# A two-layer transformer block on one core: a spread of sums one step on, a weight split ahead of the squares, one more empty step ahead of MLA's transposes

## The chip, the core and the metric

The kernel runs on one core of a Trainium2 chip. The metric is the device time of one execution in microseconds (us). The kernel before took 1670.65 us, the median of 3 runs (1670.29 to 1670.98).

Engines are named as in the profile: PE is TensorE's matmul, PEld its weight load, DVE is VectorE, ACT is ScalarE, POOL is GpSimd, SP is SyncE, which issues most of the DMAs. PSUM banks take the results of PE. Every engine takes its instructions in the order of the program.

## What is computed

Two layers of a hybrid block over 512 tokens of width 1024, in 32-bit floats. Only what the change lies near is kept here:

```python
def rms_norm(x, g):
    xf = x.astype(jnp.float32)
    y = xf * lax.rsqrt(jnp.mean(xf * xf, axis=-1, keepdims=True) + RMS_EPS)
    return (y * g.astype(jnp.float32)).astype(x.dtype)

def reference(x, w_in, ...):
    for l in range(DEPTH):
        h = rms_norm(x, g_pre_mix[l])
        mix = hybrid_mixer(h, w_in[l], ...)
        x = x + rms_norm(mix, g_post_mix[l])
        h = rms_norm(x, g_pre_ffn[l])
        f = (jax.nn.silu(h @ w_ffn_gate[l]) * (h @ w_ffn_up[l])) @ w_ffn_down[l]
        x = x + rms_norm(f, g_post_ffn[l])
    return x

def hybrid_mixer(h, w_in, ...):
    (fq, fk, fv, ff, dq, dk, dv, rq, rk, rv, rg, cq, ckv, kr) = jnp.split(h @ w_in, IN_OFFSETS, axis=-1)
    ...
    q = heads(rms_norm(cq, mla_q_norm) @ w_uq, MLA_HEADS)
    kv = heads(rms_norm(ckv, mla_kv_norm) @ w_ukv, MLA_HEADS)
    ...
```

The mixer holds four attentions (forgetting, dilated, retention, and MLA, whose queries and keys come from the small latents `cq`, `ckv`, `kr`), and gates that weigh them.

## The kernel before, in words

**Matmuls.** Every operand is split into a high part (a rounded copy) and a low part (what is left), and every product is three matmuls: high by high, high by low, low by high. For a weight, ACT makes the high part (line 290) and DVE the low part (line 291). The weights are a stream of plan entries. `w_conv(i)` splits entries up to number `i`, each by `conversion`, which first issues the load of the entry two further on (SP, line 259, three `raw` buffers) and then two casts on ACT and two subtractions on DVE. `take` hands out the next entry, with `self.wi` its number; `w_conv(self.wi)` therefore splits the entry that is to be taken next.

**Order.** Between `ordered(True)` and `ordered(False)` PE, ACT, DVE and POOL run in the order in which the code is written; elsewhere a scheduler sets the order. The written order covers the start of the program (`first_block`, `latents`) and the border of the layers (`down_block`, `latents`). SP's order is left to the scheduler at the border.

**The border of the layers.** `down_block` ends layer 0. The last of the eight columns of the FFN is computed in two halves of 256 tokens. For a half, `sums` adds the squares of the tokens on PE (line 571) and DVE makes a factor of them (lines 588 to 563); `start` spreads the factor over the partitions by two small matmuls on PE (`spread`, line 601); `renewal` then makes from it the new `x` and the split operands `u[k]` of the next layer: DVE lines 1344 and 1350, POOL line 1346, ACT line 1348. Beside it runs `latent_steps`, the product for layer 1's latents (lines 1037 to 1039): first for token blocks 0 and 1 with k from 0 to 7, six matmuls for each k, then for token blocks 2 and 3. What is done ahead of which k stands in a table `at`; the half of the first tokens is renewed by then, and the table places the sums and the spread of the second half:

```python
        at = {0: [...], 1: [...],
              EA: [lambda: sums(1), ...],
              ES: [lambda: start(1), lambda: some(g[1], 4)]}
```

with `EA, ES = 2, 5`. Token blocks 2 and 3 read the second half's operands. Once the renewal is issued, `squares()` (made by `squares_and_factors`) issues the squares of the new `x` (`square_sums`: eight squares on ACT, lines 1331 and 1334; six additions on DVE, line 1335, and one, line 1067), the split of the first `dq` weight, and an activation that loads nothing at the border but in layer 0 fetches ACT's table for the square root. `self.factors` comes in `latents` after the first of the eight k of `dq` (`TQ = 1`): it sums these squares per token on PE (line 571) and makes layer 1's factor. In the first layer `first_block` calls the same two functions with the input as `x`.

**After it.** `latents` squares the latents on ACT (line 1196), makes their factors on DVE, spreads layer 1's factor on PE (line 601, after five k of `dq` in layer 1), copies the spread on ACT (line 1076), splits the second `dq` weight, and only then scales the latents on DVE (lines 1213 to 1217).

**MLA's preparation.** `mla_prepare` is a generator that is worked off beside the columns of the projections: `collect` takes one step of the oldest background generator each time that enough columns have been issued (`SPACING = 6.5`). Its first steps split `uq` and `ukv` and rotate `kr` (DVE lines 878 to 882); the next ones transpose the latents on PE (lines 889, 895, 902). Behind it in the same queue stand MLA's attention, then the dilated, the forgetting and the retention one. In an attention, line 673 makes scores, 682 to 692 the normalised exponentials (DVE, ACT, POOL), 699 transposes them, 709 and 710 split them (ACT, DVE), 753 multiplies with the values. Scores, transposes and products take turns on the four PSUM banks named `b`.

Of the kernel before, what the change touches and what calls it, by code (L numbers as in the profile page):

```python
# [40 lines left out]


DA, DS, CQ, D0 = 4, 10, 9, 2
EA, ES = 2, 5

TQ, QT, QT1 = 1, 2, 5

# [161 lines left out]
class Builder:  # L209
# [657 lines left out]
    def mla_prepare(self, l, cq, ck, res):  # L867
        nc = self.nc
        ident = self.con("ident")
        uq = [self.split(self.up.pop(0)) for _ in range(2)]  # L870
        yield
        ukv = self.split(self.up.pop(0))
        for p in range(2):
            c = ck[p][:, 0:384].rearrange("p (t c) -> p t c", t=2)
            cs = slice(64 * p, 64 * p + 64)
            cos = self.con("tcos")[:, cs].rearrange("p (t c) -> p t c", t=2)
            sin = self.con("tsin")[:, cs].rearrange("p (t c) -> p t c", t=2)
            nc.vector.tensor_mul(c[:, :, 160:176], c[:, :, 144:160], sin[:, :, 0:16])
            nc.vector.tensor_mul(c[:, :, 176:192], c[:, :, 128:144], sin[:, :, 16:32])
            nc.vector.tensor_mul(c[:, :, 128:160], c[:, :, 128:160], cos)  # L880
            nc.vector.tensor_add(c[:, :, 160:192], c[:, :, 128:160], c[:, :, 160:192])
            nc.vector.tensor_copy(c[:, :, 128:160], c[:, :, 160:192])
        yield
        cqT, ckT = [], []
        for kb in range(2):
            tp = self.ps("b")
            for t in range(4):
                o = 256 * (t % 2) + 128 * kb
                nc.tensor.transpose(tp[:, 128 * t:128 * t + 128], cq[t // 2][:, o:o + 128], ident)
            self.defer(lambda tp=tp, kb=kb: cqT.append(self.split(tp, scale=self.vec("qn", 2 * l + kb))))  # L890
            yield
        tp = self.ps("b")
        for t in range(4):
            o = 192 * (t % 2)
            nc.tensor.transpose(tp[:, 128 * t:128 * t + 128], ck[t // 2][:, o:o + 128], ident)
        self.defer(lambda tp=tp: ckT.extend(self.split(tp, scale=self.vec("kvn", l))))
        yield
        K = [(self.ar(), self.ar()) for _ in range(4)]
        tp = self.ps("b")
        for t in range(4):  # L900
            o = 192 * (t % 2) + 64
            nc.tensor.transpose(tp[:, 128 * t:128 * t + 128], ck[t // 2][:, o:o + 128], ident)

        def shared():

            hi, lo = (t[64:128, :] for t in K[0])
            nc.scalar.copy(hi, tp[64:128, :])
            nc.vector.tensor_sub(lo, tp[64:128, :], hi.bitcast(F32))
            for h in range(1, 4):
                for p in range(2):  # L910
                    self.move(K[h][p][64:128, :], K[0][p][64:128, :])
        self.defer(shared)
        yield
        yield
        Q = []

        def q_out(ps):

            f = self.a()
            nc.vector.tensor_mul(f, ps, self.con("mrope"))  # L920
            Q.append(self.split(f))

        for h in range(4):
            ps = self.ps("b")
            for kb in range(2):
                w = [uq[kb][p][:, 128 * h:128 * h + 128] for p in range(2)]
                self.mm3(ps, w, cqT[kb], kb == 0, kb == 1)
            self.defer(lambda ps=ps: q_out(ps))
            yield
            ps = self.ps("b")  # L930
            self.mm3(ps[0:64, :], [ukv[p][:, 128 * h:128 * h + 64] for p in range(2)], ckT, True, True)
            self.defer(lambda ps=ps, h=h: self.split_to(K[h][0][0:64, :], K[h][1][0:64, :], ps[0:64, :]))
            yield
        for t in range(4):
            ts = slice(128 * t, 128 * t + 128)
            if t % 2 == 0:
                ps = self.ps("b")
            half = ps[:, 256 * (t % 2):256 * (t % 2) + 256]
            o = half.rearrange("p (h d) -> p h d", h=4)
            w = [ukv[p].rearrange("p (h d) -> p h d", h=4)[:, :, 64:128] for p in range(2)]  # L940
            nc.tensor.matmul(o, ckT[0][:, ts], w[0], start=True, stop=False)
            nc.tensor.matmul(o, ckT[0][:, ts], w[1], start=False, stop=False)
            nc.tensor.matmul(o, ckT[1][:, ts], w[0], start=False, stop=True)
            self.defer(lambda half=half: res["v"].append(self.v_split(half)))
            if t % 2 == 1:
                yield
                yield
        self.flush()
        for h in range(4):
            (q0, q1), (k0, k1) = Q[h], K[h]  # L950
            res["qk"].append(((q0, k0), (q0, k1), (q1, k0)))
# [184 lines left out]
    def squares_and_factors(self):  # L1136

        nc = self.nc
        part = []

        def squares():
            part.append(self.square_sums())
            self.w_conv(self.wi)
            nc.scalar.activation(self.small(1), part[0][:, 0:1], AF.Sqrt)
        return squares, lambda: self.next_factors(self.token_sums(part[0]))

# [865 lines left out]
```

## Time and profile before

The profiled execution took 1670.84 us, of which the span from the first to the last instruction is 1669.0 us.

| | |
|---|---|
| median of 3 runs | 1670.65 us |
| profiled execution, its span | 1670.84 us, 1669.0 us |
| busy: PE, PEld | 1647.4 us (99%), 1462.5 us (88%) |
| busy: DVE, ACT, POOL | 1135.7 us (68%), 849.8 us (51%), 357.9 us (21%) |
| chain that ended last | PE 91%, DVE 5%, issue 2%, ACT 1%, POOL 1%, DMA 1% |

PE is busy nearly all the time, so time can be gained only where PE waits, or where its clock is down. In the rows below, a time in brackets is the idle time of the engine ahead of the instruction and what ended it. The granted clock of PE is given as a share of 2.4 GHz.

### The profile page before, as it was taken

Reading aid. Unit: us, or ns where it says so; the run is one execution under the profiler, and the core shown is the slowest. Engines: PE = TensorE matmul, PEld = TensorE weight load, DVE = VectorE, ACT = ScalarE, POOL = GpSimd, SP = SyncE. Lnnn points to the kernel's source line nnn. Section 1 sums busy time; section 2 is a strip of 40 time slices with the busy share of each in tenths; the row PEclk is TensorE's granted clock in tenths of the full one; section 3 lists DMA queues with packets and bytes.
Section 4 is the critical chain, followed back from the end, with each engine's and each line's share of the span. In section 5 each row is a group of like instructions: output and inputs, shape, how many; then the busy total and the mean of one; then the engine's idle time right before and its main releaser. Section 6 shows DMA issues by size and latency. Waiting matters only on the chain.

```text
span 1669.0 us, 26499 instructions
## 1 busy us (share of the span) xinstructions
PE 1647.4 (99%) x9746; PEld 1462.5 (88%) x9746; DVE 1135.7 (68%) x2165; ACT 849.8 (51%) x1682; POOL 357.9 (21%) x400
## 2 busy tenths in 40 slices
PE   9999999999999999999999999999999999999997
PEld 7898888888899999988888988888888989999876
DVE  7657676746569777762286576767464687777897
ACT  7566553323456555553265665533333565555655
POOL 0234333432130001000122343334311300000000
PEclk9999999999999999999999999999999999999999
DMA  6645225767735777443246442257666247775572
GB/s 220 162 108 144 77 89 174 178 173 179 205 104 138 187 181 186 99 152 97 76 149 164 113 138 76 95 170 177 174 156 180 73 139 196 185 187 150 187 238 90
DMA packets 93697, 248.88 MB, mean 149 GB/s; under 512 B 11520, under 2 KB 23040, under 8 KB 93568
## 3 DMA queue, kind: packets, MB, share of 16 engines
q1 hardware_dynamic: 72768, 205.24, 39.5%
q0 software_dynamic: 20800, 41.95, 13.6%
q8 instruction: 77, 1.26, 0.3%
q14 instruction: 52, 0.43, 0.1%
HBM read 220.93 MB, written 31.46 MB: 151 GB/s over the span
## 4 chain that ended last, share of the span: by engine, by line
PE 91%; DVE 5%; issue 2%; ACT 1%; POOL 1%; DMA 1%; SPq 0%; DVEq 0%; POOLq 0%
PE acc L530 16%; PE acc L531 15%; PE acc L532 15%; PE b L504 4%; PE b L506 4%; PE b L505 4%; PE acc L504 4%; PE acc L506 4%; PE acc L505 4%; PE b L753 2%; PE b L673 2%; PE b L699 1%; PE b L1889 1%; PE b L1891 1%; PE b L1890 1%
## 5 line engine op out<-in xcount | busy, mean ns | idle before, releaser
L530 PE MATMUL acc<-a,whi 128*128 128x512 f32 (+1 forms) x1254 | 484.5, 387 | 0.0
L532 PE MATMUL acc<-a,wlo 128*128 128x512 f32 (+1 forms) x1254 | 474.6, 378 | 0.0
L531 PE MATMUL acc<-a,whi 128*128 128x512 f32 (+1 forms) x1227 | 465.0, 379 | 0.0
L290 ACT CAST whi<-raw 128x512 fp32r<-128x512 f32 (+3 forms) x398 | 213.7, 576 | 335.9 <-PE acc L531 162.3
L291 DVE TENSOR_TENSOR wlo<-raw,whi 128x512 fp32r<-128x512 f32 (+3 forms) x398 | 274.3, 718 | 121.7 <-ACT whi L290 120.8
L532 PEld LDWEIGHTS acc<-a,wlo 128*128 128x128 f32 x1254 | 236.1, 188 | 44.5
L530 PEld LDWEIGHTS acc<-a,whi 128*128 128x128 f32 x1254 | 236.8, 189 | 39.9 <-issue 1.1
L531 PEld LDWEIGHTS acc<-a,whi 128*128 128x128 f32 x1227 | 231.4, 189 | 38.7 <-issue 1.0
L406 DVE TENSOR_TENSOR wlo<-raw,whi 128x1024 fp32r<-128x1024 f32 x132 | 157.8, 1196 | 67.6 <-ACT whi L405 64.9
L405 ACT CAST whi<-raw 128x1024 fp32r<-128x1024 f32 x132 | 135.5, 1027 | 125.8 <-PE acc L505 48.9
L504 PE MATMUL acc<-a,whi 128*128 128x256 f32 x504 | 142.8, 283 | 0.3 <-DVE a L1648 0.3
L504 PE MATMUL b<-a,whi 128*128 128x256 f32 x504 | 142.7, 283 | 0.0
L506 PE MATMUL b<-a,wlo 128*128 128x256 f32 x504 | 142.6, 283 | 0.0
L505 PE MATMUL b<-a,whi 128*128 128x256 f32 x504 | 142.6, 283 | 0.0
L505 PE MATMUL acc<-a,whi 128*128 128x256 f32 x504 | 142.6, 283 | 0.0
L506 PE MATMUL acc<-a,wlo 128*128 128x256 f32 x504 | 142.5, 283 | 0.0
L1300 DVE TENSOR_TENSOR a<-acc,a 128x512 f32<-128x512 f32 x64 | 44.1, 689 | 136.2 <-PE acc L532 136.2
L334 POOL DMA_DIRECT2D raw<-wts x36 | 31.5, 876 | 344.5 <-DMA raw<-wts 113.8
L522 ACT CAST a<-a 128x512 fp32r<-128x512 f32 (+1 forms) x143 | 76.6, 567 | 50.3 <-DVE a L860 11.8
L504 PEld LDWEIGHTS acc<-a,whi 128*128 128x128 f32 x504 | 96.7, 192 | 0.6 <-DVE a L1648 0.5
L504 PEld LDWEIGHTS b<-a,whi 128*128 128x128 f32 x504 | 96.8, 192 | 0.2
L505 PEld LDWEIGHTS acc<-a,whi 128*128 128x128 f32 x504 | 96.8, 192 | 0.0
(282 smaller groups left out, 3241.1 us busy)
## 6 DMA issues: line engine op xcount, KB each, us to landing
raw<-wts SPq DMA_DIRECT2D x257, 512.0 KB, 3.7
raw<-wts POOLq DMA_DIRECT2D x36, 512.0 KB, 6.3
a<-a SPq DMA_DIRECT2D x120, 128.0 KB, 2.4
sums<-wts POOLq DMA_DIRECT2D x30, 512.0 KB, 6.4
raw<-sums SPq DMA_DIRECT2D x20, 512.0 KB, 4.3
raw<-wts SPq DMA_DIRECT2D x35, 256.0 KB, 2.8
sums<-sums POOLq DMA_DIRECT2D x10, 512.0 KB, 4.4
a<-xT SPq DMA_DIRECT2D x16, 256.0 KB, 6.2
```

Of the source, the lines that this page charges most:

```text
L290: todo.append(lambda hi=hi, src=src, n=n: nc.scalar.copy(hi[:, :n], src))
L291: todo.append(lambda hi=hi, lo=lo, src=src, n=n: (lo_engine or nc.vector).tensor_sub(lo[:, :n], src, hi[:, :n].bitcast(F32)))
L405: self.nc.scalar.copy(hi, src)
L406: self.nc.vector.tensor_sub(lo, src, hi.bitcast(F32))
L504: mm(o, hi[:, c], x[k][0], start=first, stop=False, skip_group_check=i in (2, 3, 4, 6))
L505: mm(o, hi[:, c], x[k][1], start=False, stop=False, skip_group_check=i in (2, 3, 4, 6))
L506: mm(o, lo[:, c], x[k][0], start=False, stop=k == 3, skip_group_check=i in (2, 3, 4, 6))
L522: nc.scalar.copy(hi, src)
L530: mm(out, w[0], x[0], start=start, stop=False)
L531: mm(out, w[0], x[1], start=False, stop=False)
L532: mm(out, w[1], x[0], start=False, stop=stop)
L1300: nc.vector.tensor_mul(z, ps, self.rB)
```

## The change

Three edits. `ES` goes from 5 to 6: the spread of the second half's factor, and the first four steps of its renewal, are issued ahead of k = 6 of the latents and not ahead of k = 5. In `squares`, `w_conv(self.wi)` stands ahead of `square_sums()`, so that the split of the first `dq` weight comes ahead of the squares, at the border and in the first layer. `mla_prepare` gets one more empty `yield` ahead of its transposes, in both layers; every background step behind it comes one step later. No instruction is added or taken away.

```diff
-EA, ES = 2, 5
+EA, ES = 2, 6
...
             nc.vector.tensor_add(c[:, :, 160:192], c[:, :, 128:160], c[:, :, 160:192])
             nc.vector.tensor_copy(c[:, :, 128:160], c[:, :, 160:192])
         yield
+        yield
         cqT, ckT = [], []
...
         def squares():
+            self.w_conv(self.wi)
             part.append(self.square_sums())
-            self.w_conv(self.wi)
             nc.scalar.activation(self.small(1), part[0][:, 0:1], AF.Sqrt)
```

Lines behind the new `yield` have a number that is higher by one in the kernel after (1037 becomes 1038).

**The spread, on PE at the border of the layers.** `acc_8843` and `acc_8844` are the sums of token blocks 0 and 1, `a_8777` and `a_8778` the high and low operand of k = 4, `a_8779` of k = 5. Before:

```order
L1038 MATMUL acc_8844<-wlo_8860,a_8777 128x420
L1039 MATMUL acc_8844<-whi_8859,a_8778 128x420
L601 MATMUL b_8922<-ct_79,sm2_8885 128x128 x2
L1037 MATMUL acc_8843<-whi_8859,a_8779 128x420
L1038 MATMUL acc_8843<-wlo_8860,a_8779 128x420
```

After:

```order
L1040 MATMUL acc_8844<-whi_8859,a_8778 128x420
L1038 MATMUL acc_8843<-whi_8859,a_8779 128x420
L1039 MATMUL acc_8843<-wlo_8860,a_8779 128x420
L1040 MATMUL acc_8843<-whi_8859,a_8780 128x420
L1038 MATMUL acc_8844<-whi_8859,a_8779 128x420
L1039 MATMUL acc_8844<-wlo_8860,a_8779 128x420
L1040 MATMUL acc_8844<-whi_8859,a_8780 128x420
L601 MATMUL b_8928<-ct_79,sm2_8885 128x128 x2
```

The six matmuls of k = 5 have moved ahead of the spread.

**The squares and the split, on DVE at the border of the layers**, between the last operands of the renewal and the factor of layer 1. Before:

```order
L1350 SCALAR_TENSOR_TENSOR a<-a,vt 128x256 x4
L1335 TENSOR_TENSOR a<-a 128x512 x6
L1067 TENSOR_TENSOR a<-a 128x512
L291 TENSOR_TENSOR wlo<-raw,whi 128x512 x2
L588 TENSOR_SCALAR sm_9097<-b 128x4
```

After:

```order
L1351 SCALAR_TENSOR_TENSOR a<-a,vt 128x256 x4
L291 TENSOR_TENSOR wlo<-raw,whi 128x512 x2
L1336 TENSOR_TENSOR a<-a 128x512 x6
L1068 TENSOR_TENSOR a<-a 128x512
L588 TENSOR_SCALAR sm_9097<-b 128x4
```

The two subtractions of the split have moved ahead of the seven additions; on ACT the two casts (line 290) have moved in the same way ahead of the eight squares. On SP one load of a weight (line 259), the one that takes the buffer which this split frees, has moved ahead of the three loads of `uq` and `ukv` (line 1187).

**MLA's last transposes, on PE in the first layer.** `a_342` and `a_343` hold the rotated `kr` of the token blocks; `a_124` to `a_130` are operands of k = 4 to 7 of the column beside which they run. Before:

```order
L532 MATMUL acc_536<-a_122,wlo_431 128x512
L902 MATMUL b_570<-ct_79,a_342 128x128 x2
L530 MATMUL acc_536<-a_124,whi_430 128x512
L531 MATMUL acc_536<-a_125,whi_430 128x512
L532 MATMUL acc_536<-a_124,wlo_431 128x512
L902 MATMUL b_570<-ct_79,a_343 128x128 x2
L530 MATMUL acc_536<-a_126,whi_430 128x512
```

After:

```order
L532 MATMUL acc_527<-a_126,wlo_431 128x512
L530 MATMUL acc_527<-a_128,whi_430 128x512
L531 MATMUL acc_527<-a_129,whi_430 128x512
L532 MATMUL acc_527<-a_128,wlo_431 128x512
L903 MATMUL b_579<-ct_79,a_342 128x128 x2
L903 MATMUL b_579<-ct_79,a_343 128x128 x2
L530 MATMUL acc_527<-a_130,whi_430 128x512
```

The second pair of transposes, which came after k = 4, comes after k = 6. The transposes of lines 889 and 895 move by two k as well, except that in layer 1 the three of them that stand ahead of the first column stay there.

## Rows read from the trace of the kernel before

**Rows 1.** Waits of PE: line, what it waited for, us in total, times, longest

```profile
PE b L532 <- DVE wlo L291: 1.3, 1, 1.3
PE b L673 <- DVE ptl L710: 1.1, 2, 0.6
...
PE b L601 <- DVE sm L563: 1.0, 1, 1.0
...
PE b L889 <- DVE a L1213: 0.9, 1, 0.9
...
PE b L699 <- POOL a L692: 0.6, 2, 0.3
PE b L699 <- DVE sm L682: 0.5, 2, 0.2
...
PE b L902 <- DVE a L882: 0.3, 1, 0.3
```

**Rows 2.** Timeline of PE at the border: start us, us, instruction [idle before]

```profile
842.77 0.71 PE L601 MATMUL b<-ct,sm 128*128 128x128 f32 x4 [1.00 <-DVE sm L563]
843.23 0.44 PE L1037 MATMUL acc<-whi,a 128*128 128x420 f32 x1
...
846.76 0.36 PE L1037 MATMUL acc<-whi,a 128*128 128x420 f32 x1
...
857.92 0.50 PE L532 MATMUL b<-a,wlo 128*128 128x512 f32 x1 [1.27 <-DVE wlo L291]
858.25 0.95 PE L571 MATMUL b<-ct,a 128*128 128x1 f32 x8
...
863.47 1.05 PE L601 MATMUL b<-ct,sm 128*128 128x128 f32 x8
...
867.54 0.41 PE L889 MATMUL b<-ct,a 128*128 128x128 f32 x2 [0.94 <-DVE a L1213]
```

**Rows 3.** Timeline of DVE at the border

```profile
845.31 1.00 DVE L1350 SCALAR_TENSOR_TENSOR a<-a,vt 128x256 fp32r<-128x256 f32 x1
...
852.05 4.48 DVE L1335 TENSOR_TENSOR a<-a 128x512 f32<-128x512 f32 x6 [0.54 <-ACT a L1334]
856.57 0.69 DVE L1067 TENSOR_TENSOR a<-a 128x512 f32<-128x512 f32 x1
857.18 1.29 DVE L291 TENSOR_TENSOR wlo<-raw,whi 128x512 fp32r<-128x512 f32 x2
...
865.70 1.29 DVE L291 TENSOR_TENSOR wlo<-raw,whi 128x512 fp32r<-128x512 f32 x2 [0.62 <-ACT whi L290]
```

**Rows 4.** Timeline of ACT at the border

```profile
850.88 0.61 ACT L1331 ACTIVATE a<-a 128x512 f32<-128x512 f32 x1
...
855.05 1.12 ACT L290 CAST whi<-raw 128x512 fp32r<-128x512 f32 x2
...
864.56 0.59 ACT L1076 COPY a<-b 128x512 f32<-128x512 f32 x1 [0.80 <-PE b L601]
```

**Rows 5.** Busy us (and instructions) of PE, PEld, DVE, ACT, POOL; PE clock, DMA share, GB/s

```profile
860.00:863.41 3.41, 3.41 (x9) 2.65 (x9) 1.09 (x8) 2.90 (x15) 0.00 (x0) 0.50 0.28 115
863.41:866.40 2.99, 2.99 (x18) 2.41 (x17) 1.93 (x10) 2.04 (x5) 0.00 (x0) 1.00 0.00 0
```

**Rows 6.** Timeline of SP at the border

```profile
850.87 0.91 SPq L1187 DMA_DIRECT2D a<-uq  x2
...
858.49 13.82 SPq L259 DMA_DIRECT2D raw<-wts  x3
```

**Rows 7.** Timeline of DVE in the first layer

```profile
21.52 0.69 DVE L1067 TENSOR_TENSOR a<-a 128x512 f32<-128x512 f32 x1
```

**Rows 8.** Timeline of PE in the first layer

```profile
23.95 0.95 PE L571 MATMUL b<-ct,a 128*128 128x1 f32 x8
...
44.48 0.44 PE L902 MATMUL b<-ct,a 128*128 128x128 f32 x2 [0.27 <-DVE a L882]
```

**Rows 9.** Busy us as in rows 5, in the dilated attention of the first layer

```profile
150.00:160.00 10.00, 9.44 (x60) 8.39 (x59) 8.38 (x23) 6.11 (x16) 4.64 (x6) 1.00 0.57 142
```

## The prediction, made before the changed kernel was run

> **What bounds the kernel now.** I read first the busy shares of the page, then the list of PE's waits, then the timelines of PE, DVE and ACT around each wait that the change touches, and the granted clock there. PE is busy for 99% of the span, so the reader is to look only for the places where it waits. Those that the change touches are few [rows 1]: 1.3 us for the low part of the first `dq` weight (line 532), 1.0 us for the factor of the second half (line 601), 0.9 us for the scaled latents (line 889), 0.3 us for the rotated `kr` (line 902). In the attentions beside the projections stand 1.1 us of scores that wait for a PSUM bank (line 673 behind DVE's line 710) and 0.6 and 0.5 us of transposes (line 699), each in two equal parts, one a layer. Together this is 5.7 us, a third of one per cent. A gain beyond that could come from the clock alone.
>
> The three border waits are not independent. PE waits at 842.77 for the spread, at 857.92 for the split weight, at 867.54 for the latents [rows 2], and between the first and the second of them the work that decides is DVE's and ACT's: the renewal that the spread releases, then the squares, then the sums. I therefore ask of each edit whether it moves that chain, not whether it shortens PE's wait.
>
> **Part 1, the spread a step later.** The spread waits for DVE (line 563), and nothing moves on DVE ahead of it. The 18 matmuls of k = 5 to 7 take 846.76 - 843.23 = 3.53 us [rows 2], 0.196 us each, so the six of k = 5, now ahead of the spread, take 1.18 us, about the room of the 1.00 us wait (which is counted from the end of an overlapping matmul). The wait goes, the spread stays at 842.8, and PE is 1.0 us ahead behind it. What is late next: token blocks 2 and 3. They would start 12 matmuls behind 843.23, at 845.6, and their third matmul, at 846.0, reads the low operand of k = 0, which DVE ends at 845.31 + 1.00 = 846.3 [rows 3]. So a wait of some 0.3 us comes in, and PE is 0.8 us ahead when it reaches `dq`. The renewal itself is not earlier, since the spread is not: for the chain this edit is worth 0.
>
> **Part 2, the split ahead of the squares.** ACT takes a cast or a square each 0.52 us: eight squares from 850.88 to the casts at 855.05 [rows 4]. Two casts ahead put the squares back by 1.04 us. DVE is free from 852.05 - 0.54 = 851.51; its two subtractions (1.29 us) end at 852.8, inside the time in which it now has to wait for the second square until 852.05 + 1.04 = 853.1. Its seven additions, which ended at 856.57 + 0.69 = 857.26 [rows 3], end at 858.30. PE's wait of 1.27 us for the low part goes, since that is there at 852.2. But the next thing in PE's row after three matmuls is the sum of squares (line 571), which needs the last addition: released 0.05 us after it, at 858.35, where it stood at 858.25 before [rows 2]. Queued behind it on PE is the rest of `dq`; who waits for it is DVE's factor (line 588), and behind that the whole of `latents`. So two waits of 1.00 and 1.27 us become one of about 0.3 us at token blocks 2 and 3 and one of about 2.2 us at line 571: PE would be done with the three matmuls at 857.92 - 1.27 + 0.2 - 0.8, about 856.1. The sum is +0.10 us, not -2.27.
>
> From line 571 to line 889 (858.25 to 867.54) nothing is reordered on PE, DVE or ACT, and the 0.94 us at line 889 are DVE's, not PE's: they stay, with +0.10.
>
> The same swap in the first layer: the last addition ends at 21.52 + 0.69 = 22.21 [rows 7], after the change at 23.25, and line 571 stands at 23.95 for other reasons [rows 8]. 0.7 us of cover, cost 0; a weight that has not landed when the casts ask for it, 4 us earlier, could use that up and more.
>
> On SP one load moves ahead of those of `uq` and `ukv` and waits for the end of the split's subtractions. That was 858.47 and is now 852.8, so these loads go out near 853.2, not at 850.87 [rows 6]. Their first reader stands behind 867.54: over 10 us cover it. Without that cover it would cost 2.3 us.
>
> **Part 3, the empty step.** In the first layer the last transposes come six matmuls later, at 0.17 us at the least (18 in 2.99 us, spread included [rows 5]) some 1.0 us, and what they waited for is there: -0.27 us [rows 8]. In layer 1 the list shows no such wait. The three transposes of layer 1 that wait 0.94 us keep their place ahead of the column, so that wait is not touched.
>
> Then all background steps of both mixers come one step later against the columns. No work is added, but the four small waits of each layer, 2.2 us in all [rows 1], are cast anew. They arise where DVE is 84% busy [rows 9] and a step's results come behind a weight's split. They can vanish (-2.2), or grow as much (+2.2). I take 0, between the two, since neither the amount of work nor its density changes and both layers repeat the same pattern.
>
> **The clock.** Behind the pause at 857.92 and the one-column sums the granted clock is 0.50 (1.2 GHz) from 860.00 to 863.41, then 1.00 again [rows 5]. PE does 9 matmuls in that time and loses half of 3.41 us, but little of it reaches the end: line 889 waits for DVE anyway. What reaches it is 0.62 us: the spread at 863.47 is late, ACT's copy waits 0.80 us for it [rows 4], and DVE's split behind that 0.62 us [rows 3]. In the kernel after, the pause before the sums is longer (2.2 us in one piece), so I expect the same fall and the same 0.62 us in the sum.
>
> The Trainium skill, page "TensorE: Matmul & The Clock Gate", section "HAM oscillation — how this bites in real kernels", says that PE is throttled again by pauses longer than any here. By that rule the clock would stay up, and the sum would be 0.62 us lower, 1669.9. The trace disagrees: the clock fell behind a pause of 1.27 us.
>
> **The sum.** +0.10 (border) - 0.27 (line 902) + 0 (mixers) = -0.17 us against 1670.84 us of the profiled execution (1669.0 us of span and 1.84 around it), 1670.67. That execution lies 0.19 above the median, so for the median 1670.5 us. A measurement of this kernel can tell about 0.2%, 3.3 us, from no change.
>
> **The rivals.**
>
> The change does what it seems to be for: the three border waits and that of line 902 vanish, 1.00 + 1.27 + 0.94 + 0.27 = 3.5 us, 1667.2 us. For it speak the rows of the waits alone; against it that the sum of squares needs DVE's last addition, 1.04 us later than before. Chance 0.05.
>
> The clock stays up behind the longer pause, because the pause falls otherwise in time: 0.62 us less, 1669.9 us. For it speaks that behind the 1.00 us pause at 842.77 no fall shows; against it the fall behind a shorter pause than the new one. Chance 0.15.
>
> The clock stays down twice as long: 1.7 us more are lost, less the 0.94 us in which PE waits at line 889, +0.8 us, 1671.3. The long pause and the sums together are 3.1 us of nearly idle PE. Chance 0.10.
>
> The empty step casts the mixers badly, and this is the one that ends slower than before: line 673 and line 699 wait for banks that lines 709 and 710 have yet to read, where the shift brings a weight's split on DVE ahead of them. The price is a wait like the 0.56 us one at line 673 twice more in each layer, +2.2 us, 1672.7. It decides against the change once a layer's mixer loses more than it gains at line 902, and it passes 0.2% at 1.7 us a layer. Chance 0.20, with 0.04 for over 0.2%.
>
> The forecast, with the mixers within 1 us of before: 0.50.
>
> **How the numbers follow.** The range takes the mixers' bounds to both sides, 1670.5 - 2.2 and + 2.2: 1668.3 to 1672.7. It holds the clock's cases and leaves out the full gain and the worst of the mixers. Faster by over 0.2% is the first rival, 0.05; slower by over 0.2% the tail of the last, 0.04; within 0.2% the rest, 0.91.
>
> **What would show it.** In the list of PE's waits of the kernel after: none at the border's line 601; about 0.3 us at line 1040 behind DVE's line 1351, near 846; one of 2.0 to 2.4 us at line 571 behind DVE's line 1068, ending near 858.3 less 0.3 for the first layer's gain; 0.9 us at line 889 still; none at line 903. The clock at half for 3.4 us once, behind the sums. The mixers' waits differ in place, alike in both layers. I would be wrong if line 571 is reached later than DVE's last addition, that is if the two waits vanish and do not come back there, or if a mixer's waits grow beyond 2 us.

## The result, and the profile after

The changed kernel takes 1681.41 us (median of 6 runs, 1679.77 to 1682.75), the kernel before 1670.82 us beside it on the same chip. The ratio is 1.0061, with a 95% interval of 1.0051 to 1.0070: slower by 10.6 us, beyond the range that I gave. The profiled execution took 1681.31 us with a span of 1679.5.

The first lines of the page of after, and its chain of work that ended last:

```profile
span 1679.5 us, 26473 instructions
...
PE 1653.8 (98%) x9746; PEld 1465.5 (87%) x9746; DVE 1134.5 (68%) x2165; ACT 851.0 (51%) x1682; POOL 360.7 (21%) x400
...
PE 88%; DVE 5%; DMA 3%; ACT 2%; issue 1%; POOL 1%; SPq 0%; DVEq 0%; POOLq 0%; ACTq 0%
```

The same line of the page of before:

```profile
PE 91%; DVE 5%; issue 2%; ACT 1%; POOL 1%; DMA 1%; SPq 0%; DVEq 0%; POOLq 0%
```

PE's share of the chain falls and that of the DMAs rises from 1% to 3%. That is the first hint: a transfer has come into a chain in which there was hardly one. PE's busy time, with the same 9746 matmuls, is 6 us longer, which is a hint of the clock.

PE's waits in after, to be read beside [rows 1] (line, what it waited for, us in total, times, longest):

```profile
PE b L841 <- ACT a L835: 2.7, 2, 1.6
PE b L571 <- DVE a L1068: 2.5, 2, 2.3
PE b L699 <- POOL a L692: 1.6, 4, 0.6
...
PE b L890 <- DVE a L1214: 0.9, 1, 0.9
...
PE b L673 <- DVE ptl L710: 0.8, 2, 0.6
...
PE acc L1040 <- DVE a L1351: 0.2, 1, 0.2
```

The waits at lines 601 and 532 and that of the first layer's line 902 (now 903) are gone, those at lines 1040 and 571 have come, and line 890 (889 before) keeps its 0.94 us. All this is the border as forecast. The row on top is not: line 841 did not wait at all in before, and it is not at the border. It stands in the group norm of the retention, one of the attentions that run beside the gate projections.

PE's timeline of after at the border, to be read beside [rows 2]:

```profile
846.69 0.71 PE L601 MATMUL b<-ct,sm 128*128 128x128 f32 x4
...
850.29 0.46 PE L1040 MATMUL acc<-whi,a 128*128 128x420 f32 x1 [0.21 <-DVE a L1351]
...
862.37 1.84 PE L571 MATMUL b<-ct,a 128*128 128x1 f32 x8 [2.27 <-DVE a L1068]
...
873.25 0.41 PE L890 MATMUL b<-ct,a 128*128 128x128 f32 x2 [0.94 <-DVE a L1214]
```

PE comes to the border 3.92 us late (846.69 against 842.77), stands 4.12 late at line 571 and 5.71 late at line 890. So one part of the loss is made before the border, 1.8 us in it, and the rest, to 10.5 us at the end of the span, behind it, in the second layer. Where the clock was down, in after (busy us and instructions of PE, PEld, DVE, ACT, POOL; PE clock, DMA share, GB/s):

```profile
295.57:298.98 3.41, 3.41 (x10) 2.64 (x9) 3.38 (x2) 1.14 (x2) 3.41 (x4) 0.50 1.02 268
...
1135.25:1138.66 3.41, 3.41 (x10) 2.73 (x10) 2.34 (x6) 1.77 (x3) 2.37 (x4) 0.50 0.92 210
862.18:869.01 6.83, 6.64 (x20) 5.61 (x21) 2.08 (x13) 3.88 (x19) 0.00 (x0) 0.50 0.02 6
```

In before the only fall inside the program was 3.41 us at the border [rows 5]. After has twice that time there, and one fall in each layer's retention, each right behind a wait at line 841.

**What holds line 841.** The timeline of DVE in before, at the same place of the first layer:

```profile
283.59 0.68 DVE L859 TENSOR_TENSOR a<-a,b 128x512 f32<-128x512 f32 x1
...
284.52 0.75 DVE L860 SCALAR_TENSOR_TENSOR a<-a,gnh 128x512 f32<-128x512 f32 x1
285.62 1.41 DVE L1320 SCALAR_TENSOR_TENSOR a<-a,acc 128x512 f32<-128x512 f32 x2 [0.35 <-DMA sums<-a]
...
288.15 0.68 DVE L834 TENSOR_TENSOR a<-a,b 128x512 f32<-128x512 f32 x1
...
1119.15 0.69 DVE L1320 SCALAR_TENSOR_TENSOR a<-a,acc 128x512 f32<-128x512 f32 x1
```

And that of DVE in after:

```profile
288.92 1.28 DVE L1321 SCALAR_TENSOR_TENSOR a<-a,acc 128x512 f32<-128x512 f32 x2 [3.82 <-DMA sums<-a]
...
290.72 0.68 DVE L859 TENSOR_TENSOR a<-a,b 128x512 f32<-128x512 f32 x1
...
291.92 0.74 DVE L860 SCALAR_TENSOR_TENSOR a<-a,gnh 128x512 f32<-128x512 f32 x1
292.58 0.68 DVE L834 TENSOR_TENSOR a<-a,b 128x512 f32<-128x512 f32 x1
...
1129.21 1.28 DVE L1321 SCALAR_TENSOR_TENSOR a<-a,acc 128x512 f32<-128x512 f32 x2 [4.32 <-DMA sums<-a]
```

The last row of each is the same product in the second layer. Line 1320 (1321 in after) is the gate's product. It writes in place into the gate tile `z`. Before that, `make_sums` has started a load of one value whose source is a cell of `z` (line 362, `sums<-a`); it is there only so that the sums' loads that follow do not start before the gate does. The product may not overwrite the cell until that load has landed. In before DVE has the scale of the head before (lines 859 and 860) to do meanwhile, and waits 0.35 us. In after the retention stands one step later, lines 859 and 860 come behind the product in DVE's row, and DVE stands idle for 3.82 us; in the second layer it stands idle for 4.32 us, where in before it did not wait for the load at all. All that is queued behind it is late: line 859, then line 860, then line 834, which centres the next head, then ACT's square (line 835), and for this PE waits at line 841.

The load itself on POOL's queue, in after:

```profile
279.59 1.03 POOL L334 DMA_DIRECT2D raw<-wts  x1 [5.24 <-DMA raw<-wts]
280.35 1.38 POOL L362 DMA_DIRECT2D sums<-a  x2
288.69 1.28 POOL L363 DMA_DIRECT2D sums<-wts  x2 [6.96 <-DMA sums<-a]
```

The same rows of before:

```profile
278.05 1.04 POOL L334 DMA_DIRECT2D raw<-wts  x1 [7.44 <-DMA raw<-wts]
278.97 1.22 POOL L362 DMA_DIRECT2D sums<-a  x2
285.20 1.28 POOL L363 DMA_DIRECT2D sums<-wts  x2 [5.01 <-DMA sums<-a]
```

In both it is issued behind a load of 512 KB. What waits for it goes on 6.2 us after the issue in before and 8.3 us in after.

So both ends of the hold have moved. From the issue to the product's turn on DVE it is 6.30 us in before (278.97 to 285.62 - 0.35) and 4.75 us in after (280.35 to 288.92 - 3.82); from the issue to the product's start it is 6.65 and 8.57 us. Of the 3.47 us by which the hold has grown, 1.55 are the turn that comes sooner and 1.92 the load that takes longer. The longer load comes with the step: issued on POOL in the first layer, it lands 5.8 to 6.9 us after its issue in the eight kernels here without the step, and 7.3 to 8.3 us after it in the five with one step. Why it takes longer there no run shows.

ACT's square and PE's wait in after, in the first layer and (the last row) in the second:

```profile
293.36 0.63 ACT L835 ACTIVATE a<-a 128x512 f32<-128x512 f32 x1
...
294.04 1.05 PE L841 MATMUL b<-ct,a 128*128 128x2 f32 x8 [1.12 <-ACT a L835]
...
1134.34 1.06 PE L841 MATMUL b<-ct,a 128*128 128x2 f32 x8 [1.62 <-ACT a L835]
```

The sum by the traces: 1.12 us of wait and half of 3.41 us at the low clock in the first layer, 1.62 us and the same half in the second, 6.2 us in all; 1.8 us at the border, where the clock was down for 6.83 us; of the other 2.5 us about 1.0 lies in the mixers' small waits (1.7 and 1.4 us in after, 1.1 us in each layer in before), and where the rest lies is not shown.

### The profile page after: what moved, and what is told of

It reads as the page before. It is cut to its first block, busy times and chain, and to the rows that moved or that the text cites. A ratio compares the mean times of both kernels' runs of the same rounds, so it can differ in the third digit from the quotient of the medians.

```text
span 1679.5 us, 26473 instructions
## 1 busy us (share of the span) xinstructions
PE 1653.8 (98%) x9746; PEld 1465.5 (87%) x9746; DVE 1134.5 (68%) x2165; ACT 851.0 (51%) x1682; POOL 360.7 (21%) x400
## 3 DMA queue, kind: packets, MB, share of 16 engines
q8 instruction: 77, 1.26, 0.3%
## 4 chain that ended last, share of the span: by engine, by line
PE 88%; DVE 5%; DMA 3%; ACT 2%; issue 1%; POOL 1%; SPq 0%; DVEq 0%; POOLq 0%; ACTq 0%
PE acc L530 15%; PE acc L531 15%; PE acc L532 15%; PE b L504 4%; PE b L505 4%; PE b L506 4%; PE acc L504 4%; PE acc L506 4%; PE acc L505 4%; PE b L753 2%; PE b L673 2%; PE b L699 1%; PE b L1890 1%; PE b L1892 1%; PE b L1891 1%; PE acc L1055 1%
## 5 line engine op out<-in xcount | busy, mean ns | idle before, releaser
L530 PEld LDWEIGHTS acc<-a,whi 128*128 128x128 f32 x1254 | 237.6, 189 | 39.6 <-issue 0.7
L531 PEld LDWEIGHTS acc<-a,whi 128*128 128x128 f32 x1227 | 232.2, 189 | 39.0 <-issue 0.5
L523 POOL TENSOR_TENSOR a<-a 128x512 fp32r<-128x512 f32 x40 | 59.1, 1478 | 188.3 <-ACT a L522 188.3
L504 PEld LDWEIGHTS acc<-a,whi 128*128 128x128 f32 x504 | 96.7, 192 | 0.6 <-DVE a L1649 0.5
```

The source lines that it names most:

```text
L504: mm(o, hi[:, c], x[k][0], start=first, stop=False, skip_group_check=i in (2, 3, 4, 6))
L523: (lo_engine or nc.vector).tensor_sub(lo, src, hi.bitcast(F32))
L530: mm(out, w[0], x[0], start=start, stop=False)
L531: mm(out, w[0], x[1], start=False, stop=False)
```

## The experiments

The theory that the traces suggest, A1: the empty step brings the retention behind the gate's product, which the one-value load holds up, and from this come the waits at line 841 and the clock's falls behind them. Against it stand two others: the border edits make the loss (by the long pause at line 571 and the clock), or a step more costs by itself, whatever holds DVE. Each expectation says what its letters stand for.

### The three edits one by one

The kernel before with the empty step alone (`e1_step`), with the spread alone (`e2_spread`), with the split alone (`e3_split`), and with both border edits and no step (`e4_spread_split`):

```diff
e1_step (line 883):
         yield
+        yield
e2_spread:
-EA, ES = 2, 5
+EA, ES = 2, 6
e3_split (squares(), line 1142):
-            part.append(self.square_sums())
             self.w_conv(self.wi)
+            part.append(self.square_sums())
e4_spread_split: the last two together
```

> The kernel before with the empty step ahead of MLA's transposes alone. Theory A, the empty step: the pauses at line 841 (1.12 and 1.62 us in the kernel after) and the fall of the clock behind each are its work, 2.9 us in the first layer and 3.5 in the second, and the attentions' other waits 2 us more: about 1679, with line 841 in the list of PE's waits. Theory B, the border: without the two border edits next to nothing is lost, 1670 to 1672, and line 841 doesn't wait.

> The kernel before with the spread of the second half's factor a k later alone. Both theories: PE reaches dq 0.8 us earlier and waits there for the split weight, 2.1 us in place of 1.27, line 571 stands where it stood. Theory A: 1670.8, or 1672 if the longer pause keeps the clock down for 6.8 us in place of 3.4. Theory B, that the border edits make the loss: 1674 or more.

> The kernel before with the weight split ahead of the squares alone. Both theories: the wait of 1.27 us for the split goes and one of 1.5 us at line 571 for the last addition of the squares comes, ending 0.1 us later than before. Theory A: 1670.9, one fall of the clock of 3.4 us. Theory B: 1674 or more.

> Both border edits without the empty step. Theory A: the border of the kernel after as it is there, a pause of 2.27 us at line 571 and the clock at half for 6.8 us, 1.8 us more than before: 1672.6, and nothing at line 841. Theory B: most of the 10.6 us, over 1676.

Measured: 1680.08 us for the step alone (ratio 1.0053, 1.0038 to 1.0068), 1671.49 for the spread (1.0004, 0.9995 to 1.0014), 1671.97 for the split (1.0007, 0.9998 to 1.0016), 1671.12 for both border edits (1.0004, 0.9995 to 1.0013). The step alone makes nine tenths of the loss; in its trace line 841 waits 1.45 and 1.27 us, with a fall of the clock of 3.41 us behind each:

```profile
PE b L841 <- ACT a L835: 2.7, 2, 1.5
```

The border edits change nothing that can be told, alone or together. As forecast, their waits are handed on: with the split alone line 571 waits 1.57 us; with both, line 571 waits 2.25 us and line 889 still 0.95. Two things came out otherwise than expected. With the spread alone line 532 waits 1.48 us and not 2.1. And both border edits took 1.5 us less than the 1672.6 that I gave, though their profiled execution, of 1672.30 us, shows the clock down for 6.83 us as in after. Of their ten executions the three longest (1672.30 to 1672.91 us) had a mean granted clock of 0.997 and the others (1670.64 to 1671.82 us) 0.998, so the longer fall probably does not come in every execution; only one was profiled.

### The hold taken away: a cell of its own

The changed kernel, where the one-value load reads a small copy, so that the product need not wait for it. The load stays where it is and the other loads are paced as before:

```diff
-                        self.make_sums(3 * l + gi - 1, ("pr", "qv")[dp // 2], z)
+                        when = self.sm.tile([128, 1], F32, tag="when", name="when")
+                        nc.gpsimd.tensor_copy(when, z[:, 0:1])
+                        self.make_sums(3 * l + gi - 1, ("pr", "qv")[dp // 2], when)
```

> The kernel after, but the one value that paces the sums of the weights is read from a cell of its own (one copy of 128x1 on POOL for each), not from the gate's tile; the product of line 1321 then has no read of a DMA to wait for. Theory A1, DVE is held at line 1321 by that DMA and with it the retention's steps behind it in DVE's row: the 3.8 and 4.3 us of idle ahead of line 1321 go, line 841 waits no more, the two falls of the clock in the mixers go: 1675, 6 us less than the kernel after. Rival A2, the step has brought the mean and the variance of the group norm too close for DVE and ACT anyhow: line 841 still waits over 1 us in both layers, 1680 to 1681.

Measured: 1673.16 us, 1.0016 (1.0007 to 1.0026) of before: 8.25 us come back, more than the 6 that I expected. DVE's timeline in this kernel:

```profile
284.46 0.69 DVE L1323 SCALAR_TENSOR_TENSOR a<-a,acc 128x512 f32<-128x512 f32 x1
285.82 0.69 DVE L1323 SCALAR_TENSOR_TENSOR a<-a,acc 128x512 f32<-128x512 f32 x1 [0.67 <-PE acc L532]
...
288.89 0.68 DVE L834 TENSOR_TENSOR a<-a,b 128x512 f32<-128x512 f32 x1
```

The product no longer waits for a DMA, line 834 starts at 288.89 instead of 292.58, and neither a wait at line 841 nor a fall of the clock in the mixers is left. That the load is no faster shows in the DMA issues of this stretch of 40 us (from issue to landing at the end of the row), in after and in this kernel:

```profile
sums<-a POOLq DMA_DIRECT2D x2, 0.0 KB, 8.0
```

```profile
sums<-when POOLq DMA_DIRECT2D x2, 0.0 KB, 7.4
```

7.4 us for one value against 8.0; only nobody waits for it now. Not all of the 8.25 us is the hold: in the profile of this kernel the clock at the border was down for 3.41 us and not for 6.83, which is 1.5 of the 8.8 us between the two profiles' ends.

### The hold left, and its reader put off

The changed kernel with one more step between the group norm's mean and its variance (`yield` ahead of line 838):

> The kernel after with one more empty step between the mean and the variance of the group norm. Both theories: the variance (line 842 here) stands some 6 matmuls, 1.4 us, later on PE, and its wait of 1.12 and 1.62 us goes or leaves at most 0.3. Theory A, that the falls of the clock behind it are the pause's work: they go as well, 1675. Rival, the clock falls for another reason: the falls stay, 1678.

Measured: 1672.72 us, 1.0014 (1.0004 to 1.0023), less than I expected. DVE and PE in this kernel, where the lines are one further:

```profile
289.88 1.29 DVE L1322 SCALAR_TENSOR_TENSOR a<-a,acc 128x512 f32<-128x512 f32 x2 [4.10 <-DMA sums<-a]
...
296.16 0.95 PE L842 MATMUL b<-ct,a 128*128 128x2 f32 x8
```

DVE is held for 4.10 us, longer than in after, and PE waits for none of it, since the variance stands a step later. So the hold costs nothing here once line 841 stands a step later.

### The dose: two steps, two steps without the hold, one step less

The kernel before with two empty steps (`e9_two_steps`), the same with the own cell (`e12_two_steps_cell`), the kernel before with one step less (`e10_one_less`, the `yield` of line 883 taken out), the kernel before with one step and the own cell (`e13_step_cell`), and the kernel before with the own cell alone (`e7_own_cell_before`).

> The kernel before with two empty steps more ahead of MLA's transposes. Theory A1, it is the place against the held product that counts: the group norm's scaling still stands behind line 1320 on DVE, but mean and variance come 3 matmuls later on PE than with one step, so line 841 waits 0.4 to 0.9 us; 1672 without the falls of the clock, 1677 with them. Rival, every step later costs the same again: 1688.

> The kernel before with two empty steps ahead of the retention, which took 1692.2 us, and now the own cell for the pacing load. In that run VectorE stood 7.24 us ahead of the gate's product, behind the load's landing, and TensorE 4.46 and 4.30 us at line 841, and the clock fell behind each. Theory A1 (all of that is the hold): both waits at line 841 are gone, no fall of the clock in the mixers, and 1673 to 1678 us, what is left being the small waits at lines 673, 699 and 830 of that run. Rival (a step costs by itself, whatever holds VectorE): 1685 us or more, with the wait at line 841 still there.

> The kernel before with one step less ahead of MLA's transposes. Theory A1: the scaling stands ahead of line 1320 on DVE as before, no wait at line 841, 1670 to 1673, what is lost being small waits at MLA's transposes. Rival, every step later costs the same: 1661.

> The kernel before with the one empty step, and the own cell for the pacing load: neither of the two edits at the border. The changed kernel with the own cell took 1673.2 us, and before takes 1670.8. If what is left of the 2.3 us lies in the step (small waits at lines 673 and 699 of both mixers, less the waits of the first layer that the step takes away): 1672.0 to 1673.5 us. If it lies in the border edits: 1670.3 to 1671.5 us.

> The kernel before, with the pacing load reading a cell of its own (128x1, copied on POOL) instead of the gate tile. In before the hold that this takes away cost VectorE 0.35 us, and TensorE waited for none of it. Theory A1 (the hold matters only where the retention comes a step later): 1670 to 1672 us, no difference; the copy on POOL costs nothing on TensorE. Rival (the cell by itself is a gain, so that the 8 us it gave back in the changed kernel were not the hold): 1662 to 1667 us.

Two steps took 1692.15 us (1.0126, 1.0109 to 1.0142), far more than A1 had led me to expect and near what "a step costs by itself" gave. Its trace, POOL and DVE in the first layer and then PE in both:

```profile
286.70 1.38 POOL L362 DMA_DIRECT2D sums<-a  x2
...
296.35 1.28 DVE L1320 SCALAR_TENSOR_TENSOR a<-a,acc 128x512 f32<-128x512 f32 x2 [7.24 <-DMA sums<-a]
...
302.82 1.08 PE L841 MATMUL b<-ct,a 128*128 128x2 f32 x8 [4.46 <-ACT a L835]
...
1145.44 1.86 PE L841 MATMUL b<-ct,a 128*128 128x2 f32 x8 [4.30 <-ACT a L835]
```

In the first layer the hold is 0.35, 3.82 and 7.24 us with no, one and two steps; in the second it is 0, 4.32 and 6.72 us. In the first the load has the less time to land before the product's turn comes, 6.30 us in before, 4.75 in after and 2.41 here (286.70 to 296.35 - 7.24), and it takes longer as well: from its issue to the product's start 6.65, 8.57 and 9.65 us. And where the first step's hold reached line 841 in part, that of the second adds its whole length there. With the own cell the two steps took 1678.24 us (1.0041, 1.0025 to 1.0056), and line 841 does not wait:

```profile
298.63 0.95 PE L841 MATMUL b<-ct,a 128*128 128x2 f32 x8
```

So 13.9 of the 21.3 us were the hold, and the rival's number was near for another reason than its own. But 7.4 us are left, just above what I gave (1673 to 1678 us): two steps do cost something by themselves, in small waits (line 830 waits 1.03 us in each layer, line 673 once 1.26, line 530 1.30). One step with the cell took 1672.97 us (1.0012, 1.0003 to 1.0020), the same as the changed kernel with the cell (1673.16). The 2.2 us that are left there belong to the step, then, and not to the border edits. The mixers' small waits in its trace, those of 0.15 us and more, add up to 2.0 us in the first layer and 1.2 in the second, against 1.1 in each in before. And the clock falls at another place, behind line 890, where PE has no wait for DVE left that could hide it:

```profile
868.64:872.05 3.41, 3.41 (x9) 2.67 (x8) 3.41 (x13) 2.12 (x4) 0.00 (x0) 0.50 0.33 129
```

I read the 2.2 us as these two together, which no run separates. The own cell in before, where nobody waits for the hold, took 1670.52 us (0.9996, 0.9987 to 1.0004): no difference, as A1 says. One step less took 1674.23 us (1.0023, 1.0013 to 1.0032), 1.2 us above what I expected. No line 841 waits there; the trace shows a few small waits that are new or longer (line 699 behind DVE's line 682 0.40 us in each layer, 0.23 in before; line 530 0.66 us, line 531 0.28), and a span 2.4 us longer. How the runs come to 3.8 us more than the kernel before beside them (1670.40 us) is left open.

### Why one value takes eight microseconds

The changed kernel, the load still reading `z`, but issued from ACT's queue instead of POOL's:

```diff
-            dma(d[0:1, 0:1], when[0:1, 0:1])
+            self.nc.scalar.dma_start(d[0:1, 0:1], when[0:1, 0:1])
```

> The changed kernel, with the two one-value loads of each round issued from ScalarE's queue instead of POOL's; they still read the gate tile. In the changed kernel they were issued on POOL at 280.35 and landed at 288.40 us, 0.33 us behind the 512 KB load that POOL's queue had before them. Theory A2 (they wait for that load in their queue): on a queue of its own each lands within some 2 to 3 us, VectorE's hold ahead of line 1321 is under 1 us, no wait at line 841, and 1672.5 to 1675 us. Rival (a one-value load takes that long among the other loads whatever its queue): hold and waits stay, 1680 to 1683 us.

Measured: 1674.61 us (1.0025, 1.0015 to 1.0034), 6.8 us less than the changed kernel. Its timeline on ACT's queue and on POOL:

```profile
278.67 0.73 ACTq L362 DMA_DIRECT2D sums<-a  x2
...
282.98 1.34 POOL L363 DMA_DIRECT2D sums<-wts  x2 [3.47 <-DMA sums<-a]
```

From the issue to the start of what waits for it: 282.98 - 278.67 = 4.3 us, against 288.69 - 280.35 = 8.3 us on POOL's queue. Line 841 does not wait, and DVE's product waits for PE only. That ACT's queue is another one than POOL's does not explain it by itself. In the later rounds no 512 KB load is issued on POOL just ahead of the one-value load, and there its follower starts 4.0 and 4.3 us after the issue on POOL's queue as well, here in before:

```profile
337.06 1.06 POOL L362 DMA_DIRECT2D sums<-a  x2 [4.57 <-ACT a L1301]
341.03 1.27 POOL L363 DMA_DIRECT2D sums<-wts  x2 [2.92 <-DMA sums<-a]
...
364.26 1.08 POOL L362 DMA_DIRECT2D sums<-a  x2 [4.71 <-ACT a L1301]
368.51 0.64 POOL L363 DMA_DIRECT2D sums<-sums  x1 [3.17 <-DMA sums<-a]
```

So about half of the time was the 512 KB load that stood ahead of the value in its queue; the 4.3 us also hold the time to land, among the other traffic. In the profile of this kernel the clock at the border is down for 6.83 us, as in after, so the 6.8 us are the hold without a change there; the own cell gave back 8.25, of which 1.5 lie at the border, and by these profiles the two agree. The Trainium skill, page "DMA: Bandwidth & Descriptors", section "Issuing engines are not separate DMA queues", says that issuing from several engines saves only the issuing time on the sequencer. Here it saved 4 us on one small load, and the measurement decides.

### A version that beats both

Two other edits at the border, with the step left out: the token sums start at k = 0 in the second layer, and the split of the next weight (`w_conv(self.wi)`) comes after the first scaling of the latents, not ahead of all of them. (The first expectation describes this second edit wrongly; the diff is what ran.)

```diff
@@ latents()
-            if k == TQ:
+            if k == (0 if l else TQ):
...
                 self.next_spread()
-                self.w_conv(self.wi)
...
+            if t == 0:
+                self.w_conv(self.wi)
         self.w_conv(self.wi + 1)
```

> The kernel before, with two edits to the same border that leave the retention's steps where they are: the token sums start at k = 0 in layer 1, and the second half of the latents' next weight is split after the first scaling and not after the last. The second takes away the wait of 0.94 us at line 889 and nothing else: 1669.3 to 1670.3 us. Rival (the wait is handed on to the next link, as in the runs of the single edits): 1670.5 to 1672 us. If the sums at k = 0 open a new pause at the border that the clock answers: 1672 to 1674 us.

> The kernel before, with the two border edits of the run before this one and the own cell for the pacing load. Since the hold costs TensorE nothing in before, the same as those two edits without the cell, to 0.5 us. A rival in which the cell brings a gain of its own: lower by 2 us or more.

Measured: 1669.21 us (expected 1669.3 to 1670.3), 0.9990 (0.9981 to 0.9999) of before, and with the own cell added 1669.39, 0.9990 (0.9982 to 0.9999). The clock falls once at the border in the second (3.41 us) and not in the first, so in these two profiles the gain does not hang on that. PE's waits of the first:

```profile
PE b L571 <- DVE a L1067: 1.2, 1, 1.2
PE b L902 <- DVE a L882: 1.1, 1, 1.1
```

The 0.94 us of line 889 are gone, the 1.27 us of line 532 have moved to line 571 (1.24), and the first layer's line 902 waits 0.85 us more. The gain of 1.6 us is small and its interval ends close to 1, but two kernels show it; which of the two edits brings it, no run separates. Against the changed kernel it is 12.2 us.

## Why the prediction was wrong

**Part 1, the spread: right.** No wait at line 601, 0.21 us at line 1040 behind DVE's line 1351 (forecast 0.3), and for the chain nothing, as `e2_spread` and `e4_spread_split` show.

**Part 2, the split ahead of the squares: right in its chain.** One wait of 2.27 us at line 571 behind the last addition (forecast 2.0 to 2.4), 0.20 us later against the spread than in before (forecast 0.10), and the 0.94 us at line 890 stayed. In the first layer I had put the cost at 0: line 571 waits 0.18 us there for the last addition (0.36 in `e6_own_cell`, 0.38 in `e3_split`), a small miss.

**The clock at the border: the wrong case.** I took a fall of 3.41 us and put "down twice as long" at 0.10, with +0.8 us. It came: the eight one-column sums, begun at the low clock, took 1.84 us where they had taken 0.95 [rows 2], and line 890 was reached 1.6 us later against line 571 than in before. The 0.94 us wait at line 890 hid none of this, for DVE's work ahead of it was as late as PE's: my discount of 0.94 us was the error in that price. The 0.62 us that I gave for the first 3.41 us was about right: in `e7_own_cell_before`, with the waits of before up to there and no fall, line 889 is reached 0.71 us earlier against the spread. The longer fall was no property of the edit alone, though: behind the same pause of 2.25 to 2.27 us the clock was down for 6.83 us in three kernels (after, `e4_spread_split`, `e14_own_queue`) and for 3.41 us in two (`e5_norm_step`, `e6_own_cell`).

**Part 3, the empty step: the step that failed.** The first layer's wait went, -0.27 us, as worked out. For the mixers I took "0, between -2.2 and +2.2", from the four small waits of PE's list. That bounded the cost by the waits that the list showed. But a step moves every wait of its engines, also those that end in time: DVE's 0.35 us for `DMA sums<-a` stood in the waits of DVE, too small to be read as a cost, and it was 0.35 us because lines 859 and 860 filled the rest of the load's time and the load landed 6.0 us after its issue; with the step that cover stood behind the product, and the load took 8.0 us. I named the cover of each edit at the border and asked none for the steps in the mixers, where one moved behind it. In place of 0 ± 2.2 us stand 6.2 us at line 841, its wait and the clock, and some 2 us with the step by itself (`e13_step_cell`), which alone would have been at the edge of the range (1672.97 against 1672.7). "Both layers repeat the same pattern" was true and made it worse: the loss came twice.

**The rival "casts the mixers badly"** had the right sign and the wrong place: lines 673 and 699 cost little, and line 841 was not looked at, as it had no wait in before. The sum of the prediction had no term for a clock that falls behind a new wait, and half of what was lost at line 841 is that term: 1.12 and 1.62 us of pause brought 1.7 us each on top.

## What to carry to other kernels

When a change shifts a whole stream of work by a step, list for each in-order engine the waits that are small because other work stands ahead of them, and ask what the shift brings in front of that wait, and whether what is waited for will still come as early; PE's own list does not show them. A transfer that only paces others should read a cell of its own: a read of a tile that is written again makes the transfer's whole time in its queue a condition of that writer. And price a new pause of PE of a microsecond or more at its length plus what the clock may take behind it, here 1.7 us behind each wait at line 841 of the changed kernel; behind other pauses of about that length, as the 1.00 us at line 601 of before, no fall showed.

## What the runs showed of the chip that I had not expected

A load of one value took 6.0 us (before), 8.0 us (after) and 9.2 us (two steps) from issue to landing in the first layer, where it was issued on POOL behind a 512 KB load. Its follower could start 4.3 us after the issue where it went through ACT's queue, and 4.0 to 4.3 us where it was issued on POOL with no such load just ahead.

The clock's answer to the same pauses differs from kernel to kernel. With waits of 1.00 and 1.27 us at the border before shows 3.41 us at 0.50 from 860.00, `e13_step_cell` 3.41 us from 868.64, and `e7_own_cell_before` no fall at all; with the pause of 2.25 us it was 3.41 or 6.83 us. Differences of a microsecond or two between such kernels are therefore not to be laid to an edit without a look at the clock. The Trainium skill, page "TensorE: Matmul & The Clock Gate", section "HAM oscillation — how this bites in real kernels", asks for longer pauses before the clock falls; in after it fell behind pauses of 1.12, 1.62 and 2.27 us.
